# Attention in a decoder trunk: one chain for both key heads of a tile pair, with their 64-row score products issued in turn into two banks

## The chip, the cores and the metric

The kernel runs on one core of a Trainium2 chip. The metric is the device time of one execution in microseconds, as the median of several runs. The profile is of one such execution.

## What is computed

The reference is a trunk of two decoder layers over 256 tokens of width 1024. Each layer has a feed-forward block, a token mixer (a matrix-memory branch beside sliding-window attention), a second feed-forward block and a gated input embedding. The part that matters here is the attention of 16 query heads over 4 key heads, each of 64 features, with a window of 128 tokens and a sink logit per head:

```python
scores = jnp.einsum("bnqhgd,bnkhd->bnhgqk", qb, kw) * (A_HEAD_DIM ** -0.5)
scores = jnp.where(valid[None, :, None, None], scores, -jnp.inf)
mx = jnp.maximum(jnp.max(scores, axis=-1, keepdims=True), sink)
pr = jnp.exp(scores - mx)
den = jnp.sum(pr, axis=-1, keepdims=True) + jnp.exp(sink - mx)
attn = (pr / den).astype(v.dtype)
out = jnp.einsum("bnhgqk,bnkhd->bnqhgd", attn, vw)
```

Its output `ha` goes through the product with `w_branch_a` (called ya below), is gated, and is added to the other branch.

## The kernel before

Tokens stand in two tiles of 128 (t = 0, 1). Every float32 product is carried as three products of the high and low parts of its factors, in a form that TensorE takes at full pace: high x high, high x low, low x high. Weights come from memory in 1 MB loads, ScalarE casts a part of one to its high half (`wh<-raw`), VectorE subtracts that from the whole (`wl<-raw,wh`), and eight split parts make a ring. A ninth is split only when one is dropped.

TensorE, ScalarE, VectorE and the load queue issue in the order in which the program was written out. That order comes from `Trunk` and its estimate of time, `Clock`. The big products are cut into short steps, and ahead of each `tick` (line 195) moves on those background chains whose next stage is ready by the estimate, then splits another weight part. A chain is a generator that yields wherever what follows has to wait for what it issued. `XT.wait` (line 157), called ahead of a step that reads a transposed activation, finishes the chains that still have to write it: `finish` (line 220) then issues what is left of them one stage after the other, with nothing of the waiting product in between.

In the token mixer (`mix`, line 710) the order of the big products is: kvq (keys, values and queries), v, gt (a gate), `if` (16 products for the memory's gates), ya, and then z. Of the memory branch, the chains `scans` (line 913) and `decays` (line 1000) follow `if` and run beside ya: VectorE's gate instructions, five small transposes, and four sets `wt` of products, each with three exponentials `w` behind it. The product ya is issued in two halves by its k-tiles: the first half (96 products) reads the attention output of the pair p = 0, both token tiles, and the second half (96 products) that of the pair p = 1.

The attention itself is `Swa` (line 1080). The transposed queries and keys hold a pair p of key heads in one tile of 128 partitions: head g = 0 in rows 0 to 63, g = 1 in rows 64 to 127. `groups` (line 1154) starts one chain `group` per p, t and g, eight in a layer, in the order p, t, g, as soon as its inputs are there and fewer than ACTIVE + 1 of its list are alive. The list also holds the chain `groups` itself, so ACTIVE = 5 means that up to five groups are at work.

A group does this, each step on one engine:

1. TensorE, `scores`: a mask product of 128 rows and 512 columns opens a bank `sc`, then products of 64 rows follow, three per query head. For t = 0 a bank takes four query heads of 128 keys (12 products of 128 columns), for t = 1 two of 256 keys (6 products of 256 columns), twice.
2. VectorE takes the maximum `mx`, ScalarE the exponentials `pr` with their sums `dn`, VectorE and ScalarE the sink's part `es`, and ScalarE scales `pr` by the reciprocal.
3. For each key tile s: TensorE transposes four blocks of `pr` into a bank `tp`, ScalarE casts them to `ptd` (high), VectorE subtracts (low), TensorE multiplies with the values into the bank `ha` (three products of 512 columns).
4. Behind the last `ha` set of both g, ScalarE and VectorE split the result into the place of the queries, `qT`, from where ya reads it.

In the profile all these have the line of the issuing helper, L129, so that they are told apart by the names of their tiles.

Of the kernel before, what the change touches and what calls it, by code (L numbers as in the profile page):

```python
# [12 lines left out]
F32R = mybir.dt.float32r  # L13
BF16 = mybir.dt.bfloat16
AF = mybir.ActivationFunctionType
ALU = mybir.AluOpType
# [3 lines left out]
P = 128  # L20
# [29 lines left out]
class Part:  # L50
    """k k-tiles of n weight columns, from column c0 of the raw tile: split into high and low when fed."""
# [111 lines left out]
class Trunk:  # L163
    """Every float32 product x @ w is carried as xh @ wh + xh @ wl + xl @ wh, where
    xh is x rounded to float32r and xl = x - xh, which float32r holds exactly.

    TensorE, ScalarE and VectorE issue in the order written here. The products with the weights are cut into steps
    of about 1.3 us; before each, tick() splits weights that come later and moves the chains in the background
    (norms, transposes, attention) on, so that what TensorE meets next has been ready for a while."""
# [57 lines left out]
    def defer(self, fn, *args):  # L227
        """fn(*args), once what it reads is ready; what it yields, if anything, are stages of a chain."""
# [19 lines left out]
    def consts(self):  # L248
# [11 lines left out]
        def mask(out, base, step, channel):  # L260
            """0 where base + step * column + channel * row >= 0, else NEG."""
# [23 lines left out]
    def unit(self, w, c0, n=NB):  # L285
        """Registers columns c0..c0+n of w [1024, .]."""
# [7 lines left out]
    def halves(self, src):  # L294
        """Registers two units by halves of their k-tiles; src(u, h) is a list of (raw -> view, DRAM source)."""
# [11 lines left out]
    def prefetch(self, n=RAW, cut=False):  # L307
        """Issues loads until n raw tiles are under way (cut: each in two transfers)."""
# [12 lines left out]
    def feed(self, must=False):  # L321
        """Starts to split the next weight part if it is there and the queues are short enough, or if it must."""
# [34 lines left out]
    def need(self, part):  # L357
        """Has part split before a product with it is issued."""
# [52 lines left out]
    def project_T(self, unit, xT, base):  # L411
        """(x @ unit)^T -> PSUM banks [features, 2 * T], two feature tiles in each."""
# [43 lines left out]
    def transposes(self, src, n):  # L456
        """src [P, n*128] -> PSUM [P, n, 128]."""
# [28 lines left out]
    def first_gain(self, vec):  # L486
        """The same in PSUM: products with ones, which also have TensorE's clock up when the first rows arrive."""
# [33 lines left out]
    def first_norm(self, t, g, xT):  # L521
        """The norm of the input; the first weight part's split (entry) goes between its products and its copies."""
# [36 lines left out]
    def ffn(self, xT, wg, wu, wd, sink, first=6):  # L559
# [48 lines left out]
        def last_features(c0):  # L608
            """The last features' gate and up columns side by side in one stationary tile."""
# [100 lines left out]
    def mix(self, l, xT, sink):  # L710
        """ga, gm and the merged branches carry twice their values, which the sink's scale takes back."""
# [37 lines left out]
        def job_T(units, xT, base, use, before=None):  # L749
            """use(k, ps) takes the k-tiles k, k + 1 of the transposed product [features, 2 * T]."""  # L750
# [6 lines left out]
        def gate(c0):  # L757
            """tanh(gate / 2) by k-tiles, transposed."""
# [47 lines left out]
    def per_feature(self, l):  # L806
        """Per-partition columns: conv taps (k, tile), conv bias (tile), q and k gains (both halves)."""
# [60 lines left out]
class Mlstm:  # L868
    """Matrix memory in parallel form over two blocks of 128 tokens."""
# [7 lines left out]
    def prepare(self, w_in):  # L877
        """The loads for the gates."""
# [382 lines left out]
```

## Time and profile before

| | us |
|---|---|
| median of 3 runs | 1411.66 |
| lowest and highest run | 1410.39, 1412.22 |
| span of the profiled execution | 1409.6 |
| TensorE busy | 1394.8 |
| VectorE busy | 862.7 |
| ScalarE busy | 728.0 |
| TensorE in attention's score products, 192 of 64 rows (15.6 + 12.4) | 28.0 |
| TensorE in the 24 mask products | 9.4 |

The span runs from the first to the last instruction of the execution that the profiler took; the median is of other runs, timed as a whole. Busy times of matmuls overlap, since one starts while the one before it drains. What a matmul costs is therefore read from one start to the next, or from the chain of work that ended last, which counts each stretch of time once. A timeline row gives the start, the length, the engine, the instruction with its tiles and shapes, and the count, with the idle time ahead of it and who ended that in brackets.

### The profile page before, as it was taken

The page shows a single profiled execution, that of the slowest core. Times are in us where ns is not written, and L with a number is a line of the kernel's source. Part 1 is how long each engine was busy: PE and PEld are TensorE (multiplying, and loading weights), DVE is VectorE, ACT ScalarE, POOL GpSimd, SP SyncE. Part 2 cuts the span into 40 slices and gives each one's busy share as a digit, 9 for nine tenths or more (in the row PEclk, how much of TensorE's full clock was granted, in tenths as well). Part 3 has the DMA queues.
Part 4 walks back from the last instruction along what each step waited for, and adds up shares of the span by engine and source line. Part 5 has one row for each costly group of instructions (what it writes and reads, how often), then busy time and mean ns, then how long its engine had stood idle before and what let it go on. Part 6 is the DMA issues. An engine that isn't in the chain of part 4 may idle for free.

```text
span 1409.6 us, 21951 instructions
## 1 busy us (share of the span) xinstructions
PE 1394.8 (99%) x9064; PEld 1247.4 (88%) x9064; DVE 862.7 (61%) x1209; ACT 728.0 (52%) x1136; POOL 50.1 (4%) x78
## 2 busy tenths in 40 slices
PE   8999999999999999999999999999999999999998
PEld 6999877899999889988779998778998998999876
DVE  5656457655887665454575554675658876555544
ACT  5544346765655454443554444467646654544433
POOL 0000012000000000000000000120000000000000
PEclk9999999999999999999999999999999999999999
DMA  6665645354545565565456566443545544765651
GB/s 214 220 205 174 216 138 180 109 132 151 193 151 179 165 193 196 165 232 179 164 174 206 168 209 203 147 143 104 145 150 195 172 158 162 221 193 172 204 177 60
DMA packets 125830, 243.81 MB, mean 173 GB/s; under 512 B 14977, under 2 KB 23841, under 8 KB 125730
## 3 DMA queue, kind: packets, MB, share of 16 engines
q1 hardware_dynamic: 125730, 242.41, 53.6%
q8 instruction: 71, 1.16, 0.3%
q14 instruction: 29, 0.24, 0.1%
HBM read 241.34 MB, written 1.05 MB: 172 GB/s over the span
## 4 chain that ended last, share of the span: by engine, by line
PE 95%; DMA 2%; DVE 2%; ACT 1%; issue 0%; POOL 0%; SPq 0%; ACTq 0%
PE dn L129 17%; PE pg L129 15%; PE pu L129 14%; PE gt L129 7%; PE z L129 6%; PE gu L129 6%; PE kvq L129 5%; PE ya L129 3%; PE v L129 3%; PE ym L129 3%; PE og L129 3%; PE yo L129 3%; PE tp L129 3%; PE sc L129 2%; PE ha L129 1%; DVE wl L129 1%
## 5 line engine op out<-in xcount | busy, mean ns | idle before, releaser
L129 DVE TENSOR_TENSOR wl<-raw,wh 128x1024 fp32r<-128x1024 f32 x448 | 541.4, 1222 | 371.0 <-ACT wh L129 367.8
L129 ACT CAST wh<-raw 128x1024 fp32r<-128x1024 f32 x448 | 461.9, 1049 | 422.9 <-PE dn L129 92.4
L129 PE MATMUL dn<-wh,hid 128*128 128x512 f32 x688 | 219.2, 397 | 0.0
L129 PE MATMUL pg<-uT,wh 128*128 128x256 f32 x1088 | 194.7, 281 | 0.0
L129 PE MATMUL pu<-uT,wh 128*128 128x256 f32 x1088 | 193.8, 280 | 0.0
L129 PEld LDWEIGHTS pg<-uT,wh 128*128 128x128 f32 x1088 | 167.2, 189 | 0.2
L129 PEld LDWEIGHTS pu<-uT,wh 128*128 128x128 f32 x1088 | 167.2, 189 | 0.0
L129 PEld LDWEIGHTS dn<-wh,hid 128*128 128x128 f32 x688 | 129.2, 188 | 32.4 <-issue 2.9
L129 PE MATMUL pu<-uT,wl 128*128 128x256 f32 x544 | 153.3, 282 | 0.0
L129 PE MATMUL pg<-uT,wl 128*128 128x256 f32 x544 | 153.3, 282 | 0.0
L129 PE MATMUL dn<-wl,hid 128*128 128x512 f32 x352 | 140.6, 399 | 0.0
L129 PEld LDWEIGHTS pg<-uT,wl 128*128 128x128 f32 x544 | 102.3, 188 | 0.0
L129 PEld LDWEIGHTS pu<-uT,wl 128*128 128x128 f32 x544 | 102.3, 188 | 0.0
L129 PE MATMUL gt<-uT,wh 128*128 128x256 f32 x512 | 93.7, 284 | 0.0
L129 PE MATMUL z<-uT,wh 128*128 128x256 f32 x512 | 92.3, 282 | 0.0
L129 PE MATMUL gu<-wh,uT 128*128 128x512 f32 x256 | 83.9, 404 | 1.7 <-ACT uT L129 1.7
L129 PEld LDWEIGHTS dn<-wl,hid 128*128 128x128 f32 x352 | 66.1, 188 | 19.5 <-issue 5.3
L129 PEld LDWEIGHTS gt<-uT,wh 128*128 128x128 f32 x512 | 78.9, 189 | 1.3
L129 PEld LDWEIGHTS z<-uT,wh 128*128 128x128 f32 x512 | 78.6, 188 | 0.2
L129 PE MATMUL z<-uT,wl 128*128 128x256 f32 x256 | 72.0, 281 | 0.0
L129 PE MATMUL gt<-uT,wl 128*128 128x256 f32 x256 | 71.9, 281 | 0.0
L129 PE MATMUL kvq<-wh,uT 128*128 128x512 f32 x192 | 63.4, 400 | 0.0
(188 smaller groups left out, 2057.4 us busy)
## 6 DMA issues: line engine op xcount, KB each, us to landing
raw<-in_w_in_dram SPq DMA_DIRECT2D x60, 1024.0 KB, 4.9
raw<-in_ffn_w_up_dram SPq DMA_DIRECT2D x40, 1024.0 KB, 5.0
raw<-in_ffn_w_down_dram SPq DMA_DIRECT2D x40, 1024.0 KB, 5.1
raw<-in_ffn_w_gate_dram SPq DMA_DIRECT2D x39, 1024.0 KB, 5.1
raw<-in_w_branch_a_dram SPq DMA_DIRECT2D x16, 512.0 KB, 5.8
raw<-in_w_branch_m_dram SPq DMA_DIRECT2D x8, 1024.0 KB, 4.9
raw<-in_w_out_dram SPq DMA_DIRECT2D x8, 1024.0 KB, 4.9
raw<-in_ple_gate_w_dram SPq DMA_DIRECT2D x8, 1024.0 KB, 5.9
```

The lines of the kernel that those rows point to most:

```text
L129: return issue(*args, **kw)
```

## The change

The two chains of a tile pair, one per key head, become one chain `pair` per p and t, four in a layer. Its score products for the two heads are issued in turn: first the two mask products, then for each query head and each of the three products the one of g = 0 (rows 0 to 63) into the first bank, the one of g = 1 (rows 64 to 127) into the second. The maxima, exponentials, sums and scalings of the two heads follow in one chain, the heads one after the other, and the transposes and `ha` sets go g by g and s by s. ACTIVE goes from 5 to 2. As the chain `groups` is in the list still, up to two pairs are at work. The number of instructions stays. Comments are dropped throughout.

```diff
-ACTIVE = 5              # attention groups at work at a time
+ACTIVE = 2
...
-                for g in range(2):
-                    while sum(c in tr.bg for c in chains) > ACTIVE:
-                        yield
-                    chains.append(tr.start(self.group(t, p, g, acc)))
-                    self.haT.written(chains[-1], 4 * p, 4, t)
+                while sum(c in tr.bg for c in chains) > ACTIVE:
+                    yield
+                chains.append(tr.start(self.pair(t, p)))
+                self.haT.written(chains[-1], 4 * p, 4, t)
...
         def scores(j0):
-            ps = tr.bank("sc").rearrange("p (j s) -> p j s", j=per)
-            mask = tr.band[:, 2 * P - S :]
-            nc.tensor.matmul(ps, tr.identb, mask[:, None, :].to_broadcast([P, per, S]), start=True, stop=False,
-                             skip_group_check=True)
+            ps = [tr.bank("sc").rearrange("p (j s) -> p j s", j=per) for _ in range(2)]
+            for g in range(2):
+                nc.tensor.matmul(ps[g], tr.identb, mask, start=True, stop=False, skip_group_check=True)
             for j in range(per):
                 for x, y in ((0, 0), (0, 1), (1, 0)):
-                    nc.tensor.matmul(ps[:, j, :], self.qT[x](4 * p + j0 + j, tok, p=rows), self.kT[rows, y, p, :S],
-                                     start=False, stop=x == 1, skip_group_check=True)
+                    for g in range(2):
+                        nc.tensor.matmul(ps[g][:, j, :], self.qT[x](4 * p + j0 + j, tok, p=rows[g]),
+                                         self.kT[rows[g], y, p, :S], start=False, stop=x == 1, skip_group_check=True)
             return ps
...
         for j0 in range(0, 4, per):
             ps = scores(j0)
+            js = slice(j0, j0 + per)
             yield
-            yield from weights(j0, ps)
...
+            for g in range(2):
+                nc.vector.tensor_reduce(mx[g][:, js], ps[g], axis=AX.X, op=ALU.max)
+                nc.vector.scalar_tensor_tensor(mx[g][:, js], mx[g][:, js], -0.125, self.nsink[:, hd[g]][:, js],
+                                               op0=ALU.mult, op1=ALU.min)
+                yield
+                for j in range(per):
+                    i = j0 + j
+                    nc.scalar.activation(pr[g][:, i, :], ps[g][:, j, :], AF.Exp, scale=0.125, bias=mx[g][:, i : i + 1],
+                                         accum_out=den[g][:, i : i + 1])
...
+        out, n, total = None, 0, 2 * (t + 1)
+        for g in range(2):
             for j in range(4):
-                nc.tensor.transpose(ps[:, j * P : (j + 1) * P], pr[:, j, s * P : (s + 1) * P], tr.ident)
+                nc.scalar.mul(pr[g][:, j, :], pr[g][:, j, :], den[g][:, j : j + 1])
             yield
-            ptd = tr.slot("ptd", F32R)[:, : 2 * NB].rearrange("p (x n) -> p x n", x=2)
-            yield from tr.splitting(ptd[:, 0], ptd[:, 1], ps)
-            yield
...
+            for s in range(t + 1):
+                ps = tr.bank("tp")
+                for j in range(4):
+                    nc.tensor.transpose(ps[:, j * P : (j + 1) * P], pr[g][:, j, s * P : (s + 1) * P], tr.ident)
+                yield
+                ptd = tr.slot("ptd", F32R)[:, : 2 * NB].rearrange("p (x n) -> p x n", x=2)
+                yield from tr.splitting(ptd[:, 0], ptd[:, 1], ps)
+                yield
+                out = out or tr.bank("ha")
+                tr.mm3(out, self.vpad[s, 0][:, 2 * p + g, :], self.vpad[s, 1][:, 2 * p + g, :], ptd[:, 0], ptd[:, 1],
+                       n == 0, n == total - 1)
+                n += 1
```

The first place is TensorE's order at the first scores of the first layer (p = 0, t = 0). Before, one head's bank `sc` is opened by its mask and filled:

```order
L129 MATMUL kvq_2218<-wh_2137,uT_113 128x512
L129 LDWEIGHTS identb
L129 MATMUL sc_2308<-band,identb 128x512
L129 MATMUL sc_2308<-kT_1989,qT_130 128x128 x2
L129 MATMUL sc_2308<-kT_1989,qT_132 128x128
```

Now two banks are opened, and the products alternate between them:

```order
L129 MATMUL kvq_2218<-wh_2137,uT_113 128x512
L129 LDWEIGHTS identb
L129 MATMUL sc_2312<-band,identb 128x512
L129 LDWEIGHTS identb
L129 MATMUL sc_2313<-band,identb 128x512
L129 MATMUL sc_2312<-kT_1989,qT_130 128x128
L129 MATMUL sc_2313<-kT_1989,qT_130 128x128
```

The second bank's mask product has moved ahead of the first bank's score products, and each of these has one of the other rows behind it.

The second place is TensorE's order around the last `ha` set of the first layer, which ends the chain p = 1, t = 1. The tiles `qT_130` and `qT_132` hold the output of p = 0 (high and low), `qT_131` and `qT_133` that of p = 1. Before, the set stands within the first half of ya, 42 of whose products are ahead of it and 54 behind:

```order
L129 MATMUL ya_3178<-qT_132,wh_2946 128x256
L129 MATMUL ya_3178<-qT_130,wl_2947 128x256
L129 MATMUL ha_3075<-ptd_3201,vpad_1987 128x512 x3
L129 MATMUL ya_3179<-qT_130,wh_2946 128x256
L129 MATMUL ya_3179<-qT_132,wh_2946 128x256
```

Now four sets of transposes and four `ha` sets stand between the last `wt` set and the second half of ya:

```order
L129 MATMUL wt_3309<-mask_st,identb 128x128
L129 MATMUL tp_3324<-ident,pr_3079 128x128 x4
L129 MATMUL ha_3332<-ptd_3329,vpad_1985 128x512 x3
L129 MATMUL tp_3336<-ident,pr_3079 128x128 x4
L129 MATMUL ha_3332<-ptd_3341,vpad_1987 128x512 x3
L129 MATMUL tp_3351<-ident,pr_3080 128x128 x4
L129 MATMUL ha_3332<-ptd_3356,vpad_1985 128x512 x3
L129 MATMUL tp_3362<-ident,pr_3080 128x128 x4
L129 MATMUL ha_3332<-ptd_3367,vpad_1987 128x512 x3
L129 MATMUL ya_3115<-qT_131,wh_2896 128x256
L129 MATMUL ya_3115<-qT_133,wh_2896 128x256
```

The whole end of that chain has moved behind the first half of ya. Its first scores have moved too: before, the last two score banks of the layer were issued among the products of gt; now one pair of banks stands right behind `if` and the other among the first half of ya.

The third place is ScalarE's order for the same chain end. Before, the last cast of `ptd` and the cast of the result stand between the memory's gates and weight parts:

```order
L129 CAST ptd_3201<-tp_3185 128x512
L129 ACTIVATE gates_3175<-gates_3175 4x256
L129 ACT_TABLE_LOAD
L129 ACTIVATE gates_3175<-gates_3175 4x256
L129 CAST wh_3233<-raw_3097 128x1024
L129 CAST qT_131<-ha_3075 128x4x128
```

Now the chain's scaling, four casts and the cast of the result follow the last `w` exponentials:

```order
L129 ACTIVATE w_3300<-wt_3309,gcols_3178 128x128 x3
L129 ACTIVATE pr_3079<-pr_3079,dn_3083 128x256 x4
L129 CAST ptd_3329<-tp_3324 128x512
L129 CAST ptd_3341<-tp_3336 128x512
L129 ACTIVATE pr_3080<-pr_3080,dn_3084 128x256 x4
L129 CAST ptd_3356<-tp_3351 128x512
L129 CAST ptd_3367<-tp_3362 128x512
L129 CAST qT_131<-ha_3332 128x4x128
```

They have moved behind the `w` exponentials of all four `wt` sets, and the scaling of the second head stands between the casts. The second layer's order is like the first's in all three places.

More of the change, by code (lines that the diff above doesn't have):

```diff
@@ L1154, in groups @@
     def groups(self, chains):
-        tr, acc = self.tr, {}
+        tr = self.tr
         for p in range(2):
@@ L1160, in groups, with pair @@
                     yield
[L1161 to L1167 removed]
+                while sum(c in tr.bg for c in chains) > ACTIVE:
+                    yield
+                chains.append(tr.start(self.pair(t, p)))
+                self.haT.written(chains[-1], 4 * p, 4, t)
+    def pair(self, t, p):
         tr, nc = self.tr, self.nc
@@ L1171, in group @@
         per = NB // S
-        rows = slice(g * AD, (g + 1) * AD)
         tok = slice(t * P, (t + 1) * P)
-        hd = slice(4 * (2 * p + g), 4 * (2 * p + g) + 4)
-        pr = tr.slot("pr")[:, : 4 * S].rearrange("p (j s) -> p j s", j=4)
-        mx, den, es = tr.col("mx", 4), tr.col("dn", 4), tr.col("es", 4)
+        rows = [slice(g * AD, (g + 1) * AD) for g in range(2)]
+        hd = [slice(4 * (2 * p + g), 4 * (2 * p + g) + 4) for g in range(2)]
+        pr = [tr.slot("pr")[:, : 4 * S].rearrange("p (j s) -> p j s", j=4) for _ in range(2)]
@@ L1178, in scores @@
+        mx, den, es = ([tr.col(n, 4) for _ in range(2)] for n in ("mx", "dn", "es"))
+        mask = tr.band[:, 2 * P - S :][:, None, :].to_broadcast([P, per, S])
         def scores(j0):
-            ps = tr.bank("sc").rearrange("p (j s) -> p j s", j=per)
-            mask = tr.band[:, 2 * P - S :]
-            nc.tensor.matmul(ps, tr.identb, mask[:, None, :].to_broadcast([P, per, S]), start=True, stop=False,
-                             skip_group_check=True)
+            ps = [tr.bank("sc").rearrange("p (j s) -> p j s", j=per) for _ in range(2)]
+            for g in range(2):
+                nc.tensor.matmul(ps[g], tr.identb, mask, start=True, stop=False, skip_group_check=True)
@@ L1205, in group @@
+        for g in range(2):
+            nc.vector.tensor_tensor(es[g], mx[g], self.sink[:, hd[g]], op=ALU.add)
         yield
-        nc.scalar.activation(es, es, AF.Exp)
+        for g in range(2):
+            nc.scalar.activation(es[g], es[g], AF.Exp)
         yield
-        nc.vector.tensor_tensor(den, den, es, op=ALU.add)
-        nc.vector.reciprocal(den, den)
+        for g in range(2):
+            nc.vector.tensor_tensor(den[g], den[g], es[g], op=ALU.add)
+            nc.vector.reciprocal(den[g], den[g])
@@ L1210, in group @@
         yield
-        for j in range(4):
-            nc.scalar.mul(pr[:, j, :], pr[:, j, :], den[:, j : j + 1])
-        yield
-        total = 2 * (t + 1)
-        for s in range(t + 1):
-            ps = tr.bank("tp")
-            for j in range(4):
-                nc.tensor.transpose(ps[:, j * P : (j + 1) * P], pr[:, j, s * P : (s + 1) * P], tr.ident)
-            yield
-            ptd = tr.slot("ptd", F32R)[:, : 2 * NB].rearrange("p (x n) -> p x n", x=2)
-            yield from tr.splitting(ptd[:, 0], ptd[:, 1], ps)
-            yield
-            if (t, p) not in acc:
-                acc[t, p] = [tr.bank("ha"), 0]
-            out, n = acc[t, p]
-            acc[t, p][1] += 1
-            tr.mm3(out, self.vpad[s, 0][:, 2 * p + g, :], self.vpad[s, 1][:, 2 * p + g, :], ptd[:, 0], ptd[:, 1],
-                   n == 0, n == total - 1)
@@ L1235, in tile_trunk @@
+        yield
+        yield from tr.splitting(self.haT[0](4 * p, tok, 4), self.haT[1](4 * p, tok, 4),
+                                out.rearrange("p (j t) -> p j t", j=4))
 @with_exitstack
```

18 lines of the change are left out of this document (3 added, 15 removed).

## The prediction, made before the changed kernel ran

> **What bounds the kernel now.** I read the page first: the busy times and the chain of work that ended last.
>
> ```profile
> PE 1394.8 (99%) x9064; PEld 1247.4 (88%) x9064; DVE 862.7 (61%) x1209; ACT 728.0 (52%) x1136; POOL 50.1 (4%) x78
> PE 95%; DMA 2%; DVE 2%; ACT 1%; issue 0%; POOL 0%; SPq 0%; ACTq 0%
> ```
>
> TensorE sets the end. A busy share over the whole span says nothing of one stage, so the second view was the busy time by stretches of the attention part of the first layer (columns: stretch, its length, busy time of PE, PEld, DVE, ACT, POOL, then the granted clock, DMA share and GB/s).
>
> ```profile
> 230.00:260.00 30.00, 30.00 (x165) 23.44 (x164) 21.36 (x47) 21.24 (x61) 3.54 (x10) 1.00 0.42 139
> 260.00:290.00 30.00, 30.00 (x175) 24.77 (x173) 17.81 (x32) 23.65 (x64) 0.00 (x0) 1.00 0.28 76
> 290.00:320.00 30.00, 30.00 (x239) 29.14 (x239) 18.82 (x34) 19.75 (x37) 0.95 (x1) 1.00 0.61 150
> 320.00:345.00 25.00, 25.00 (x190) 22.07 (x189) 14.45 (x21) 12.84 (x22) 0.00 (x0) 1.00 0.46 152
> ```
>
> TensorE has no gap here at all. So two things count and nothing else does: TensorE time that the change saves in this part, and TensorE idle time that it makes there. Both go into the end one for one. By the order of instructions the streams of TensorE are alike ahead of the first scores of a layer and again from the first z product on, so everything happens between these two places, once per layer.
>
> **Part 1, the score products in turn.** The timeline of TensorE, around the first four score banks (start, length, instruction, count), its weight loads in the same place, and the chain of work that ended last:
>
> ```profile
> 235.17 0.39 PE L129 MATMUL sc<-band,identb 128*128 128x512 bf16 x1
> 235.49 1.55 PE L129 MATMUL sc<-kT,qT 64*128 64x128 f32 x12
> 236.97 0.39 PE L129 MATMUL sc<-band,identb 128*128 128x512 bf16 x1
> ...
> 239.58 0.39 PE L129 MATMUL sc<-band,identb 128*128 128x512 bf16 x1
> 239.90 0.97 PE L129 MATMUL sc<-kT,qT 64*128 64x256 f32 x6
> 240.81 0.39 PE L129 MATMUL sc<-band,identb 128*128 128x512 bf16 x1
> ```
>
> ```profile
> 235.49 1.41 PEld L129 LDWEIGHTS sc<-kT,qT 64*128 64x128 f32 x12 [0.23 <-ACT sq L129]
> ```
>
> ```profile
> 235.33 3.52 PE sc L129 x26
> 239.74 2.37 PE sc L129 x14
> 467.77 21.54 PE yo L129 x93
> ```
>
> A 128-column product costs (236.97 - 235.49) / 12 = 0.123 us, a 256-column one (240.81 - 239.90) / 6 = 0.152. The mask product ahead of them takes 0.32 to the next start (235.17 to 235.49); a full-array product of 512 columns in a row of its like takes 21.54 / 93 = 0.232, so 0.09 is the price of going from 128 rows to 64. Two groups of token tile 0 take 3.52 us on the chain, two half-groups of token tile 1 take 2.37.
>
> The trace of before has no two neighbouring products on different rows of the array, so what turn by turn brings is bounded. If two neighbours run at once, a pair costs what one costs: 0.23 + 0.32 + 12 x 0.123 = 2.03 for token tile 0, which saves 1.49; 0.23 + 0.32 + 6 x 0.152 = 1.46 for token tile 1, which saves 0.91. Ahead of the ya products there are per layer two of each: 4.8 us, 9.6 for both layers. If the weight loads still go one behind the other, at the pace of the row of loads (twelve in 1.41 us with the last one's 0.19 in it, 0.11 to 0.12 each), the pair for token tile 0 stays at 0.55 + 24 x 0.123 = 3.50 and the other becomes 0.55 + 12 x 0.118 = 1.97: per layer 2 x 0.02 + 2 x 0.40, 1.7 for both. Below zero: if each change of rows cost the 0.09 of the change from 128 rows, 2 x 24 x 0.09 + 2 x 12 x 0.09 = 6.5 per layer would be added. Nothing excludes that, but both kinds are already 64-row products, so I keep it as a rival only. No row lies nearer to one of the gaining ends, so I take their middle, 5.7 us. The Trainium skill, "TensorEngine Tiling (Array Packing)", Key Properties, says that tiles work independently and can load weights and multiply in parallel, while changing the tiling mode drains TensorE. By this rule the gain would be the upper end and the sum 3.9 us lower; the 0.09 us at the mask agrees with its drain, and no run here shows the parallel part yet.
>
> The two pairs of the last chain stand between the ya products, where TensorE waits for others in any case (part 2), so I count nothing for them (at most 4 x 0.91 = 3.6 for both layers).
>
> **Part 2, the order that follows.** With two chains at a time, the last one (p = 1, token tile 1) starts its scores only after the `if` products, and the second half of ya needs its result. Before, the last ha set stood among the first half of ya, with 54 ya products behind it. In the changed order four steps stand with nothing between them: 4 transposes, ha, 4 transposes, ha, and so on, then ya. Each step is a chain through three engines. Its prices, from the timelines of PE, ACT and DVE (in brackets the idle time before and who ended it), and what TensorE itself needs, from the chain:
>
> ```profile
> 314.17 0.60 PE L129 MATMUL tp<-ident,pr 128*128 128x128 f32 x4
> ...
> 319.55 0.86 PE L129 MATMUL ha<-ptd,vpad 128*128 128x512 f32 x3
> ```
>
> ```profile
> 296.26 0.59 ACT L129 CAST qT<-ha 128x512 fp32r<-128x512 f32 x1 [2.33 <-PE ha L129]
> ...
> 306.84 0.56 ACT L129 CAST ptd<-tp 128x512 fp32r<-128x512 f32 x1
> ...
> 314.86 0.59 ACT L129 CAST ptd<-tp 128x512 fp32r<-128x512 f32 x1 [1.57 <-PE tp L129]
> ...
> 320.45 0.59 ACT L129 CAST qT<-ha 128x512 fp32r<-128x512 f32 x1 [1.33 <-PE ha L129]
> ```
>
> ```profile
> 296.87 0.69 DVE L129 TENSOR_TENSOR qT<-ha,qT 128x512 fp32r<-128x512 f32 x1 [2.77 <-ACT qT L129]
> ...
> 307.44 0.69 DVE L129 TENSOR_TENSOR ptd<-tp,ptd 128x512 fp32r<-128x512 f32 x1 [0.85 <-ACT ptd L129]
> ```
>
> ```profile
> 313.64 0.69 PE ha L129 x3
> 314.33 0.44 PE tp L129 x4
> ```
>
> From the first transpose to the cast 0.69 (314.17 to 314.86), cast to subtraction 0.60 (306.84 to 307.44), subtraction 0.69: at 1.98 the second of the three ha products can go, and with two at 0.23 the next transposes start at 2.44. TensorE's own work in that is 0.69 + 0.44 = 1.13, so a step idles 1.31, four of them 5.2 us. Behind the last one comes the cast of the output, 0.90 after the first of three unbroken products (319.55 to 320.45), so 0.44 after the third, then 0.61 to the subtraction (296.26 to 296.87) and 0.69 of it: 1.98 + 0.23 + 0.44 + 0.61 + 0.69 = 3.95 from the step's start, of which 2.44 is in the step: 1.5 more. Between the second and the third step ScalarE also scales the second head's four weights; its 1.71 (below) fits beside the subtraction and ha but for about 0.2.
>
> What stands ahead of the first step:
>
> ```profile
> 330.62 1.05 PE wt L129 x4
> ```
>
> ```profile
> 292.22 1.71 ACT L129 ACTIVATE pr<-pr,dn 128x256 f32<-128x256 f32 x4 [0.97 <-DVE dn L129]
> ...
> 331.71 0.88 ACT L129 ACTIVATE w<-wt,gcols 128x128 f32<-128x128 f32 x3 [2.36 <-PE wt L129]
> ```
>
> In the changed order TensorE issues the last wt set and then the transposes; ScalarE stands at three w exponentials of that wt, which start as the set ends (331.67, 331.71) and take 0.88, and behind them four scalings, 1.71. The last transpose waits for the last scaling, so TensorE idles at least 0.04 + 0.88 + 1.71 less three transposes at 0.11, 2.3. ScalarE comes there with much else behind it (eight exponentials of scores, nine of w, four weight casts within the 96 ya products), so it may be later still; I take 2.7 and up to 5.
>
> At the start of ya the first product needs the subtraction of the ha set that stands right behind `if`. VectorE has gate work and a weight subtraction in front of it, and ScalarE a table load in front of the next cast:
>
> ```profile
> 313.68 0.47 DVE L129 TENSOR_SCALAR gates<-if,m_igate_b 4x256 f32<-4x256 f32 x1 [2.12 <-PE if L129]
> ...
> 315.92 1.21 DVE L129 TENSOR_TENSOR wl<-raw,wh 128x1024 fp32r<-128x1024 f32 x1
> ```
>
> ```profile
> 316.46 1.28 ACT L129 ACT_TABLE_LOAD   x1
> ```
>
> From the end of `if`: 0.2, 2.24 for the gates, 1.21 and 0.69 make 4.3, against TensorE's own two ha sets, four transposes and a score pair, 2 x 0.69 + 0.44 + 2.37 = 4.2 (3.3 if the pair overlaps). With the next ha set behind the table load this is between 0 and 2 us; I take 1.
>
> So a layer idles 1 + 2.7 + 5.2 + 0.2 + 1.5 = 10.6 us, both 21.2. It isn't given back: in before no stretch of this part has a wait that an earlier TensorE stall could fill, and the ring of eight weight parts only stands full when ya goes on. The count of all instructions stays, the weight transfers (SP's queue) only stand a little earlier against them, and VectorE and ScalarE have room (61% and 52%), so the moved max, exponential and scaling work costs nothing outside the waits above.
>
> **The sum.** The profiled execution has a span of 1409.6; the runs' median of 1411.66 is 2.1 more. Span: 1409.6 + 21.2 - 5.7 = 1425.1; time: 1427.2.
>
> **The rivals.** *The products don't overlap, chance 0.20.* For it: the pace of 0.123 at 128 columns looks like the loads' pace, not the columns'. Gain 1.7 instead of 5.7: 1431.2.
>
> *The clock falls in the wait, 0.14.* The last TensorE product of before starts at 1404.15; the granted clock is still full in the next stretch and half in the one after:
>
> ```profile
> 1404.15 0.39 PE L129 MATMUL pg<-wh,uT 128*128 128x512 f32 x1
> ```
>
> ```profile
> 1406.00:1408.00 2.00, 0.00 (x0) 0.00 (x0) 0.62 (x1) 0.00 (x0) 0.00 (x0) 1.00 0.26 103
> 1408.00:1409.60 1.60, 0.00 (x0) 0.00 (x0) 0.00 (x0) 0.00 (x0) 0.00 (x0) 0.52 0.09 35
> ```
>
> So about 3.5 us idle halve it. The wait ahead of the first step is 2.3 to 5. Price: the parts of four steps on the chain doubled, 4 x (0.44 + 0.46) = 3.6, and some 3.5 us of ya at half speed, 1.8: 5.4 per layer, 10.8 for both: 1438.0. Against it: 2.7 is under 3.5, and each step has products. The Trainium skill, "TensorE: Matmul & The Clock Gate", Part 1, gives an idle window of about 3.4 us for the fall and as long a busy one for the rise; the end of the trace agrees with the first.
>
> *Changing rows drains the array, 0.06.* 13 us are added, none gained: 1411.66 + 21.2 + 13 = 1445.9.
>
> *Faster, 0.06.* The pairs overlap everywhere, also between the ya products: 9.6 + 3.6 = 13.2. That decides once a layer idles less than 6.6, so with ScalarE ahead of TensorE at the first step (no 2.7, no 1) and steps shorter by a third, as would be if the 0.69 to the cast were mostly ScalarE's own lateness there: 2 x 4.7 - 13.2 = -3.8, 1407.9. Against it: ScalarE's 1.57 of idle time ended by just those transposes. In between, no change has 0.04.
>
> **How the numbers follow.** The forecast (waits of 10 us a layer, part of the overlap) has 0.50 and gives 1427.2. Low end: no extra lateness, 2 x (2.3 + 5.2 + 1.5) = 18.0 less 9.6 gives 1420; with steps a third shorter and all overlap counted it goes to about 1415, which I take. High end: 2 x (5 + 6.9 + 2) = 27.8 without gain, 1439.5; the clock's 1438.0 lies in it; I take 1441. Within 0.2% (2.8 us, about what measurements of this kernel can tell) lies only the in-between case: same 0.04, faster 0.06, slower 0.90.
>
> **What would show it.** Right: TensorE's waits list shows tp for ACT, ha for DVE and ya for DVE, some 10 us a layer between `if` and z, where before lists none; a pair for token tile 0 takes 2.0 (overlap) or 3.5 us (none). Wrong: those waits sum to under 4 us a layer, or the pair takes over 3.6, or the granted clock leaves 1.00 there.

## The result, and the profile after

| | before | after |
|---|---|---|
| median (lowest to highest), us | 1411.66 (1410.39 to 1412.22) | 1429.59 (1428.48 to 1430.36) |
| span of the profiled execution, us | 1409.6 | 1426.7 |
| mean granted clock there | 0.999 | 0.985 |

The changed kernel is slower: the medians differ by 17.9 us, or 1.3%, where 15.5 us had been forecast. The ratio on record is 1.0116, with a 95% interval of 1.0095 to 1.0137, which holds the medians' 1.0127. The forecast of 1427.2 was close, but two of its parts were wrong by some 8 and 10 us, in opposite directions. The mean clock already points to one of them.

The page of the changed kernel (busy times, then the granted clock in 40 slices):

```profile
PE 1400.3 (98%) x9064; PEld 1245.5 (87%) x9064; DVE 862.1 (60%) x1209; ACT 727.5 (51%) x1136; POOL 51.8 (4%) x78
PEclk9999999997999999999999999999889999999999
```

TensorE is busy 5.5 us longer with the same instructions, and the clock falls in slice 10 (321 to 357 us) and in slices 29 and 30: the ends of the two layers' attention. These are its waits (waiting engine and tile, engine and tile waited for, sum, count, longest; two at the start of the kernel are left out):

```profile
PE ha L129 <- ACT ptd L129: 5.4, 8, 0.7
PE tp L129 <- DVE xn L129: 3.8, 2, 2.4
PE tp L129 <- ACT pr L129: 2.7, 2, 1.4
PE tp L129 <- DMA p<-in_p_dram: 2.5, 2, 2.2
...
PE ya L129 <- DVE qT L129: 1.6, 2, 0.8
PE ya L129 <- ACT qT L129: 1.4, 2, 0.7
```

The tiles are those of the prediction: `tp` waits for the scaling, `ha` for the casts, `ya` for the output. But they sum to 5.4 + 2.7 + 1.6 + 1.4 = 11.1 us, 5.5 a layer where 10 had been expected. The rest hides in busy time, as the timeline of TensorE at the end of the chain shows:

```profile
321.49 1.52 PE L129 MATMUL tp<-ident,pr 128*128 128x128 f32 x4 [1.37 <-ACT pr L129]
323.68 1.95 PE L129 MATMUL ha<-ptd,vpad 128*128 128x512 f32 x3 [0.68 <-ACT ptd L129]
325.43 1.05 PE L129 MATMUL tp<-ident,pr 128*128 128x128 f32 x4
327.16 1.95 PE L129 MATMUL ha<-ptd,vpad 128*128 128x512 f32 x3 [0.68 <-ACT ptd L129]
...
336.73 1.30 PE L129 MATMUL ya<-qT,wh 128*128 128x256 f32 x2 [0.68 <-ACT qT L129]
```

A step takes 327.16 - 323.68 = 3.48 us, not 2.44. Three unbroken `ha` products had taken 0.86; these take 1.95. The busy times by stretches say why (the granted clock is the third number from the end):

```profile
315.00:320.00 5.00, 5.00 (x30) 3.07 (x29) 2.36 (x4) 4.61 (x18) 0.00 (x0) 1.00 0.13 49
320.00:325.00 5.00, 2.75 (x9) 1.34 (x7) 1.40 (x6) 3.21 (x10) 0.00 (x0) 0.81 0.67 210
325.00:330.00 5.00, 4.28 (x13) 2.54 (x11) 0.69 (x1) 2.20 (x6) 0.00 (x0) 0.50 0.01 3
330.00:335.00 5.00, 3.70 (x9) 2.13 (x10) 1.38 (x2) 1.16 (x2) 0.00 (x0) 0.50 0.00 0
335.00:340.00 5.00, 4.18 (x15) 3.17 (x16) 0.69 (x1) 0.59 (x1) 0.00 (x0) 0.50 0.00 0
340.00:345.00 5.00, 5.00 (x43) 5.00 (x43) 2.33 (x3) 1.64 (x2) 0.00 (x0) 0.98 0.00 0
```

The clock is half from 323.1 to 340.2 us, through all four steps and the first ya products, and again for 20.5 us in the second layer. Products at half clock look like work in a list of waits, so that list understates the loss.

The score products went the other way. The timeline at the first pair, and the pairs on the chain of work that ended last:

```profile
234.83 0.61 PE L129 MATMUL sc<-band,identb 128*128 128x512 bf16 x2
235.37 1.55 PE L129 MATMUL sc<-kT,qT 64*128 64x128 f32 x24
236.85 0.50 PE L129 MATMUL kvq<-wh,uT 128*128 128x512 f32 x1
```

```profile
234.99 1.93 PE sc L129 x26
...
237.82 1.35 PE sc L129 x14
...
275.21 1.93 PE sc L129 x25
...
311.13 1.33 PE sc L129 x14
```

24 products now take 236.85 - 235.37 = 1.48 us, what 12 took before: the overlap is full. On the chain a pair for token tile 0 costs 1.93 us and one for token tile 1 1.35. The forecast's bounds (2.03 and 3.50, 1.46 and 1.97) were added up from one start to the next; read in that way the first two pairs take 236.85 - 234.83 = 2.02 and 239.10 - 237.66 = 1.44. In the profile of before the layer's eight groups take 16.2 us on the chain, now 2 x 1.93 + 4 x 1.34 = 9.2. That is 7.0 a layer, 14 for both, of which 3.7 lie in the last chain, for which nothing had been counted. (One of its pairs stands behind `if`, off the chain; it is taken to be as long as the other.) The Trainium skill, "TensorEngine Tiling (Array Packing)", Key Properties, says that tiles work independently and can load weights and multiply in parallel; the trace agrees, with 24 products in 1.48 us.

So there are three things to settle by experiment. Is the loss all in the order that ACTIVE = 2 makes? Is the gain due to the other rows, to the other bank, or to both? And how much is the clock, and what makes it fall, since TensorE stood idle nowhere in this part for 3.5 us?

One thing is needed to read the times below: on the chips of the experiments the clock also fell in some executions of the kernel before, which took 1410.2 to 1419.9 us at mean clocks of 1.000 to 0.992. Each ratio is against its runs on the same chip; the arithmetic between kernels uses executions at a clock of 1.00 where it says so.

### The profile page after: what moved, and what is told of

The parts are those of the page before. It is cut to its first block, busy times and chain, and to the rows that moved or that the text cites. A ratio compares the mean times of both kernels' runs of the same rounds, so it can differ in the third digit from the quotient of the medians.

```text
span 1426.7 us, 21932 instructions
## 1 busy us (share of the span) xinstructions
PE 1400.3 (98%) x9064; PEld 1245.5 (87%) x9064; DVE 862.1 (60%) x1209; ACT 727.5 (51%) x1136; POOL 51.8 (4%) x78
## 3 DMA queue, kind: packets, MB, share of 16 engines
q8 instruction: 71, 1.16, 0.3%
## 4 chain that ended last, share of the span: by engine, by line
PE 95%; DMA 2%; DVE 1%; ACT 1%; issue 0%; SPq 0%; ACTq 0%
PE dn L129 17%; PE pg L129 15%; PE pu L129 14%; PE gu L129 7%; PE z L129 6%; PE gt L129 6%; PE kvq L129 5%; PE ya L129 4%; PE ym L129 3%; PE v L129 3%; PE yo L129 3%; PE og L129 3%; PE tp L129 3%; PE ha L129 2%; PE sc L129 1%; DMA raw<-in_ffn_w_gate_dram 1%
```

## Experiments: the order

**Four chains at a time.** The changed kernel with one number changed:

```diff
-ACTIVE = 2
+ACTIVE = 4
```

> The changed kernel with ACTIVE = 4, so that all four pairs of a layer may be at work and the last one's scores are issued among the gt products again. Theory A (the loss is the order: the last chain stands alone ahead of the second half of ya, and the half clock follows from that idle time; the overlap itself saves 16.2 - 9.3 = 6.9 us a layer): no waits of TensorE between the first scores and z, clock 1.00 there, 1411.7 - 13.9 = 1397 to 1400 us. Rival B (the pair chain itself makes the wait, since its two heads go one after the other): 1420 us or more, with the same waits ahead of ya. Rival C (the overlap is given back elsewhere, in ScalarE or in PSUM banks): 1408 to 1412 us.

Measured: 1401.23 us (1399.57 to 1403.66), ratio 0.9894 (0.9879 to 0.9910). The slowdown is gone, and the kernel is faster than before. An execution at a clock of 1.00 took 1399.57. All of the last chain but its last `ha` set is done while ya's first half runs. That set stands behind the half, and the waits of TensorE between 300 and 340 us are down to these:

```profile
PE ya L129 <- ACT qT L129: 0.7, 1, 0.7
PE ya L129 <- DVE qT L129: 0.3, 1, 0.3
```

This is the whole sum without the chain's end: 1411.66 less 14 of overlap, plus twice 1.0, gives 1399.7. The loss of the change lay in ACTIVE = 2, not in the pairing. The profile, which is of the slowest of the four executions (1403.66 us), still has half clock behind these waits, for 3.4 us in the first layer and 6.8 in the second.

**A quarter of z ahead of ya.** 96 of a layer's 384 z products, which need nothing from the attention, are put ahead of ya, so that the chain's end stands among them and the first ya products (both layers, with ACTIVE = 4):

```diff
+        rec.qk_job(w_in, 0, 0)
...
-        for part in range(2):
-            rec.qk_job(w_in, part, 0)
+        rec.qk_job(w_in, 1, 0)
```

> ACTIVE = 4, in turn, and the first z product (96 products with uT, which waits for no attention) is issued ahead of ya instead of behind it, so that the last ha set stands 100 products ahead of the second half of ya. Theory A: the 1.0 us a layer that TensorE waited for ACT and DVE at ya is gone, and with it the windows of half clock there (1 in layer 1, 2 in layer 2): 1395 to 1398 us. Rival G (the half clock comes from the wt products beside, not from the wait): half clock still, 1399 to 1402 us. Rival H (the memory branch loses its cover when z moves): over 1402 us.

Measured: 1396.75 us (1395.66 to 1397.82), ratio 0.9862 (0.9840 to 0.9884). No wait of ya is left in the list, and the clock is half for only one stretch of 3.4 us, at 700.6, in the input embedding. This is the best version, and it beats both kernels.

## Experiments: what overlaps

**The banks one after the other.** The changed kernel, but each bank filled on its own behind the two masks:

```diff
-            for j in range(per):
-                for x, y in ((0, 0), (0, 1), (1, 0)):
-                    for g in range(2):
+            for g in range(2):
+                for j in range(per):
+                    for x, y in ((0, 0), (0, 1), (1, 0)):
```

> The changed kernel, but each bank's products issued in one go, first those of head g = 0, then those of g = 1; the rest of the order as in the changed kernel. Theory A (neighbours on different rows run at once): the pairs go back to 3.4 and 2.3 us; those ahead of ya count in full, 2 x (2 x 1.5 + 2 x 0.95) = 9.8 us, the others by up to 3.8: 1439 to 1443 us. Rival (the saving came from two mask products in a row and fewer changes between 128 and 64 rows, 0.09 us each): at most 1432 us.

Measured: 1434.89 us (1432.51 to 1435.64), ratio 1.0132 (1.0115 to 1.0149), 5.3 above the changed kernel. Neither expectation held, and the chain shows the reason:

```profile
234.23 2.88 PE sc L129 x26
...
238.01 1.70 PE sc L129 x14
```

Without turns a pair should have taken 3.5; it takes 2.88. The recorded starts are 0.11 us apart, except at the seam, where seven follow each other after 0.05 to 0.06 us in the mean: the last four or so products of the first head and the first four of the second lie in one another. The records don't name the head, but products of this width on the same rows start 0.11 us apart everywhere else, so the close starts must alternate between the rows. By this reading TensorE starts products on the other rows ahead of products on its present rows that are written before them, about four places ahead. A third of a bank's twelve overlaps without turns, if nothing with 128 rows stands at the seam. With the four pairs a layer that stand well ahead of ya, 2 x (2 x 0.95 + 2 x 0.35) = 5.2, near the 5.3 measured. That it is so near is in part luck: in the profiles the two stretches from the first scores to z are 7.2 us longer, with half clock for 3.4 us more in the first layer, and the rest of the program is 3.2 us shorter.

The same with ACTIVE = 4, where the order costs nothing:

> ACTIVE = 4 and each bank's products in one go: the pair chain with neither the turn by turn nor the late last chain. Theory A: within 3 us of the kernel before, 1409 to 1414 us, no waits ahead of ya. Rival B (the pair chain costs by itself): 1416 us or more.

Measured: 1408.88 us (1406.87 to 1417.82), ratio 0.9962 (0.9942 to 0.9983). At a clock of 1.00 it took 1407.0, 7.4 above the 1399.57 of ACTIVE = 4; all pairs by the chain give 2 x (2 x 0.95 + 4 x 0.35) = 6.6.

**A mask between the heads.** With ACTIVE = 4, the second mask product moved behind the first head's products, so that a product of 128 rows stands at the seam, as before the change:

```diff
-            for g in range(2):
-                nc.tensor.matmul(ps[g], tr.identb, mask, start=True, stop=False, skip_group_check=True)
             for g in range(2):
+                nc.tensor.matmul(ps[g], tr.identb, mask, start=True, stop=False, skip_group_check=True)
                 for j in range(per):
```

> ACTIVE = 4, and the two heads' scores apart as in the kernel before: mask and products of g = 0, then mask and products of g = 1, so that a 128-row product stands between the two row halves. Theory A' (products of the two row halves run at once, in turn for the whole pair, and at the seam for about four products ahead where no 128-row product stands between): no two starts closer than 0.1 us, a pair at 3.5 and 2.3 us again, and over the run with ACTIVE = 4 in turn all of 2 x (2 x 1.59 + 4 x 1.0) = 14 us, 1412 to 1416 us. Rival (the early starts in the run with whole banks came from something else, as the order of loads): a pair under 3.0 us here too, at most 1410 us.

Measured: 1425.52 us (1423.19 to 1431.80), ratio 1.0073 (1.0047 to 1.0099). The pairs came out as expected, at the price of before; the time did not:

```profile
235.64 3.52 PE sc L129 x26
...
240.05 2.37 PE sc L129 x14
...
249.98 7.46 PE sc L129 x40
```

A mask at the seam is enough to undo all of the overlap. By the chain, the pairs are 0.64 and 0.67 longer than in the run before this one: 1407.0 + 2 x (2 x 0.64 + 4 x 0.67) = 1415, so some 10 us are unexplained by the products. The clock was half for 30.7 us, which can cost up to half of that, 15.4 us, if TensorE has no wait to fill there. This is where it first fell:

```profile
250.45:253.86 3.41, 3.41 (x27) 2.81 (x26) 0.00 (x0) 2.08 (x5) 0.00 (x0) 1.00 0.03 5
253.86:257.27 3.41, 3.41 (x13) 2.63 (x13) 1.84 (x5) 0.00 (x0) 0.00 (x0) 0.50 0.00 0
```

TensorE had been busy for every one of the 3.41 us ahead of the fall, with nothing but masks and 64-row products. No idle time is needed; this is taken up below.

**The other bank or the other rows.** With ACTIVE = 4, in each layer's first pair the products of one head alternate between two banks, on the same rows, and then those of the other head; the four masks are half as wide:

```diff
...
+            for g in range(2):
+                for h in range(2):
+                    nc.tensor.matmul(banks[g][h], tr.identb, mask[:, :2], start=True, stop=False,
+                                     skip_group_check=True)
+                for j in range(2):
+                    for x, y in ((0, 0), (0, 1), (1, 0)):
+                        for h in range(2):
+                            nc.tensor.matmul(banks[g][h][:, j, :], self.qT[x](4 * p + 2 * h + j, tok, p=rows[g]),
...
```

> ACTIVE = 4, products in turn, but the first pair of each layer (p = 0, token tile 0) has its heads one after the other and each head's products alternate between two banks with the same rows. Theory A' (it is the other rows, not the other bank): starts 0.11 us apart within a head, so the two heads' 24 products take 2.6 to 3.0 us, against 1.48 in turn by rows. Rival F (another bank is enough): starts in pairs and 1.5 us. Elsewhere as with ACTIVE = 4.

One execution: 1406.76 us. The first pair of each layer, on the chain:

```profile
235.69 3.68 PE sc L129 x28
```

```profile
930.39 3.52 PE sc L129 x28
```

In the first layer the clock falls to half at 238.90, within the pair. At full clock, in the second layer, the pair takes the 3.52 us of before, and within a head no two starts are closer than 0.108 us. The bank brings nothing; the rows do.

## Experiments: the clock

**Unread products against the fall.** The changed kernel with 25 mask products a layer whose results nobody reads: 8 ahead of the first transposes, 3 behind each set, 5 ahead of ya:

```diff
+        last = p == 1 and t == 1
+        full = tr.band[:, None, :].to_broadcast([P, 2, 2 * P])
+
+        def warm(bank, times):
+            for _ in range(times if last else 0):
+                tr.tc.nc.tensor.matmul(bank.rearrange("p (j s) -> p j s", j=2), tr.identb, full, start=True, stop=True,
+                                       skip_group_check=True)
...
+                if n == 0:
+                    warm(ps, 8)
...
+                if last:
+                    spare = tr.bank("warm")
+                    warm(spare, 3)
...
+        if last:
+            warm(spare, 5)
```

> The changed kernel with extra mask products that nothing reads, in TensorE's idle time of the last chain of each layer: eight ahead of its first transposes, three behind each set of transposes, five ahead of the second half of ya (25 a layer, 0.23 us each). The order of all else is the same. Theory A (the half clock costs 5 to 6 us a layer on top of the waits): the clock stays at 1.00, a step takes 2.4 to 2.5 us instead of 3.47, 1417 to 1421 us. Rival D (the steps are bound by ScalarE and VectorE, the half clock costs nothing): 1428 to 1432 us, whatever the clock shows. Rival E (the products come too late or are too thin to hold the clock): clock 0.50 still, 1429 us or more.

Measured: 1418.29 us (1417.27 to 1420.63), ratio 1.0030 (1.0015 to 1.0046), with the clock at 1.00 throughout in the profile. With more work the kernel is 11.3 us faster than the changed one (9.9 between the two profiled executions). It also shows the waits at full clock. One step on the chain:

```profile
324.91 0.45 PE tp L129 x4
325.38 0.59 ACT ptd L129
326.00 0.70 DVE ptd L129
326.75 0.73 PE ha L129 x2
327.48 0.49 PE tp L129 x4
```

2.57 us from one set of transposes to the next, for a forecast of 2.44. Transposes, cast, subtraction and two `ha` products, each waiting for the one before: the step was read rightly.

**Only the eight ahead of the first step:**

> The changed kernel with only the eight unread mask products ahead of the last chain's first transposes (8 of the 25 of the run with all of them). It tells where the clock falls. Theory J (the wait ahead of the first step lets it fall, the steps themselves keep what they find): clock 1.00, 1418 to 1421 us. Rival K (the steps, with 1.3 us idle in each 2.4, let it fall by themselves): clock 0.50 from the second or third step on, 1425 to 1430 us.

Measured: 1424.04 us (1421.10 to 1424.87), ratio 1.0055 (1.0037 to 1.0073). The first fall is put off from 323.1 to 326.3 us in the first layer, but the steps by themselves then let the clock fall, for 13.7 and 17.1 us. Neither expectation was met fully: the long wait is not the only cause, and where it is filled the loss is smaller.

**A count of the use.** With ten profiles at hand I took the moments at which the granted clock changes. In each profile they lie on a grid of 3.413 us (323.09, 715.62 and 1026.24 in the changed kernel are 115 and 91 such stretches apart), so every stretch of the grid can be looked at. For each I summed the products' columns, at the 0.232 us per 512 columns of the chain, each product weighed by its rows over 128, so that one of 64 rows counts half. With the two runs below there are twelve profiles. They give, for stretches at full clock from the first clock record (13 to 17 us) to the last product:

| use of a stretch, columns x rows | stretches | followed by half clock |
|---|---|---|
| under 0.35 | 17 | 17 |
| 0.35 to 0.45 | 21 | 6 |
| over 0.45 | 4794 | 0 |

Counted by columns alone, without the rows, nothing separates them: 12 of the 82 stretches between 0.35 and 0.70 were followed by a fall. The stretch ahead of the fall in the changed kernel (319.68 to 323.09) has a use of 0.10. A step at full clock has 0.93 us of products in 2.44 to 2.57, 0.36 to 0.38: on the edge. At half clock it has 0.93 in 3.48, 0.27, and stays there until ya runs. And a score pair as before the change, 12 + 12 products of 64 rows and two masks, has 1.16 us of full use in 3.52, 0.33: when a stretch of the grid falls on it whole, as at 235.49 in the profile with the same rows and at 250.45 with the mask between, the clock falls. That would also explain why the kernel before varies from 1410 to 1420, but this is not shown, since no profile of one of its slower executions was taken. Two runs test the count.

**One unread product per step instead of three** (17 a layer):

> The changed kernel with unread mask products as in the run warm, but one behind each set of transposes instead of three (8 ahead of the first set and 5 ahead of ya as there, about 17 a layer). Theory U (use): the clock is set anew every 3.41 us by how much TensorE worked in the 3.41 us before, a product counting its columns times its rows over 128. In the profiles so far every such stretch with under a third of the full pace (512 columns in 0.232 us) was followed by half clock, none with over 0.44. A step of 4 transposes and 3 ha products is 0.93 us of products; with one of 0.23 more, in a step of about 2.5 us, the use is 0.46: the clock stays at 1.00 and the time is that of warm or a little below, 1417 to 1420. Rival V (gaps): the clock falls because TensorE stands still about 1 us in each step; one product more leaves a gap of that size: half clock in both layers, 1423 to 1430.

Measured: 1420.07 us (1417.77 to 1421.50), ratio 1.0043 (1.0027 to 1.0058). The time is that of the upper end expected for the use, 1420. TensorE now waits in each step, and the clock holds. These are two stretches of this profile's grid, with a use of 0.37 and 0.46; the first lies where both outcomes occur, so the run speaks against the gaps rather than for an exact bound:

```profile
321.22:324.63 3.41, 2.59 (x10) 1.15 (x9) 0.69 (x1) 1.56 (x4) 0.00 (x0) 1.00 0.82 289
324.63:328.04 3.41, 2.64 (x14) 1.37 (x12) 0.69 (x1) 2.44 (x6) 0.00 (x0) 1.00 0.00 0
```

**All 25, but on 32 rows instead of 128**, so that they take as long and count a quarter (against the run with 25):

```diff
-                tr.tc.nc.tensor.matmul(bank.rearrange("p (j s) -> p j s", j=2), tr.identb, full, start=True, stop=True,
+                tr.tc.nc.tensor.matmul(bank.rearrange("p (j s) -> p j s", j=2), tr.identb[:32], full[:32], start=True, stop=True,
...
```

> The run warm (25 unread mask products a layer in the same places), but each of them on 32 rows instead of 128, with the same 512 columns, so that TensorE is busy as long but works on a quarter of the rows. Theory U (use, a product counting columns times rows): the first 3.41 us hold 8 products of 0.23 at a quarter and four transposes, 0.46 + 0.23 = 0.7 us or a use of 0.2, so the clock falls ahead of the steps; a step then has 0.93 + 0.17 in about 3.6 us, 0.31, and it stays at half: 1427 to 1433. Rival B (busy time): what counts is whether TensorE runs anything: the clock stays at 1.00 as in warm, 1417 to 1421.

Measured: 1435.46 us (1434.29 to 1435.76), ratio 1.0147 (1.0119 to 1.0175). The stretch ahead of the fall, with a use of 0.24, and the two behind it:

```profile
319.40:322.81 3.41, 3.34 (x16) 1.25 (x14) 1.25 (x5) 3.16 (x12) 0.00 (x0) 1.00 0.45 106
322.81:326.22 3.41, 3.41 (x10) 1.84 (x10) 0.69 (x1) 0.58 (x1) 0.00 (x0) 0.50 0.53 202
326.22:329.64 3.42, 3.42 (x10) 1.57 (x9) 0.69 (x1) 2.19 (x5) 0.00 (x0) 0.50 0.00 0
```

TensorE is busy 3.34 of 3.41 us, and the clock falls; with one product of 128 rows per step it is busy 2.59 and 2.64 of 3.41, and the clock stays. It is not the idle time that counts but columns times rows. The time is above the expected 1427 to 1433, since the clock was half for 20.5 and 23.9 us, longer than in the changed kernel, and the unread products too take twice as long there.

## Why the prediction was right in its number and wrong in two parts

In the terms of its own sum, with the same 1411.66 as start:

| term, both layers | forecast | measured | from |
|---|---|---|---|
| score products | -5.7 | -14 | chain, 16.2 to 9.2 a layer |
| waits at full clock | +21.2 | +20.6 | warm: 1418.29 + 14 - 1411.66 |
| half clock | 0 | +11.3 | changed kernel less warm |
| sum | 1427.2 | 1429.6 | |

Two of the measured terms are differences of medians from different chips, and the sum comes out by construction. The profiles check them. From the first score bank of a layer to its first z product the two layers take 107.8 and 107.8 us before, 110.8 and 110.9 with the unread products, and 115.2 and 116.2 in the changed kernel. So the half clock costs 4.4 + 5.3 = 9.7 us there, and the waits 6.1 + 14 = 20.1. The remaining 1.3 us of the difference of the spans lie outside these stretches.

- **The waits: right.** With the clock kept up, the two layers lose 20.6 us by the medians and 20.1 by the profiles, if the unread products cost nothing there. In the first layer of that run it can be read directly: from 319.72, the start of the unread products behind the last `wt` set, to the second ya product at 334.05 are 14.3 us, of which four steps' own work is 4 x 1.13 and one ya product 0.12. That leaves 9.7; the forecast for the same part was 2.7 + 5.2 + 0.2 + 1.5 = 9.6. Ahead of the first ya half TensorE waited 0.8 a layer, forecast 1. That the list shows only 5.5 a layer comes from the half clock, in which the products fill part of their own wait.
- **The overlap: right in its mechanism, mis-sized.** "No row lies nearer to one of the gaining ends, so I take their middle, 5.7 us" failed: the upper end was the true one, with 10.3 us instead of 9.6 for the pairs ahead of ya. Nearly all of the 0.7 between them is a slip in the working and no further overlap: it subtracted a length from start to start (2.03, measured 2.02) from one on the chain (3.52), where the same two groups count 0.09 less than from start to start (235.17 to 238.78, 3.61). And "I count nothing for them", of the last chain's two pairs, failed as well: 3.7 us. One of the pairs stands among ya products and not in a wait; the other stands ahead of ya, whose wait the sum holds with the pair already overlapped. The argument for the lower end, that 0.123 us is the pace of the loads, was true of loads on the same rows only: in the changed kernel two loads start 3 ns apart. The rival "the products don't overlap" fell with it, and so did "changing rows drains the array": the 23 changes of rows among a pair's 24 products cost nothing that can be seen.
- **The clock: wrong.** It was kept as a rival at 0.14, and came true. The step that failed is "about 3.5 us idle halve it", with its conclusion "2.7 is under 3.5, and each step has products". TensorE's longest idle time here was 1.37 us. What the end of the trace showed was one case of low use, taken for a rule on idle time. The price was about right: 5.4 per layer, 10.8 for both, where the medians give 11.3 and the profiles 9.7. The Trainium skill, "TensorE: Matmul & The Clock Gate", Part 1, has a free-running window of 3413 ns, which the grid agrees with; it has the fall after an idle window, and there the measurement decides: windows with 100% of busy time were followed by half clock when their use was under 0.35.
- **The first step's wait: right in its cause, a little shorter.** From the end of the `wt` set at 320.1 to the last transpose at 322.68 are 2.6 us, less three transposes 2.2, at the low end of the forecast's 2.3 to 5, of which it took 2.7. ScalarE's rows show the queue that was named: the `w` exponentials, then the scalings.

```profile
319.10 0.88 ACT L129 ACTIVATE w<-wt,gcols 128x128 f32<-128x128 f32 x3
...
320.16 0.88 ACT L129 ACTIVATE w<-wt,gcols 128x128 f32<-128x128 f32 x3
320.92 1.70 ACT L129 ACTIVATE pr<-pr,dn 128x256 f32<-128x256 f32 x4
```

- **By its own test of being wrong**, "the granted clock leaves 1.00 there", the forecast's case did not happen. Full overlap, the forecast's waits and the rival's clock together would have given 1411.66 + 21.2 - 14 + 10.8 = 1429.7. That the number 1427.2 was close is luck: an under-counted gain and a left-out loss nearly cancelled.

## What to carry to other kernels

Two 64-row products on different halves of the rows run at once if they follow each other closely and no product on all rows stands between them; a chain that is made longer for this needs enough other chains at work, or its end stands bare. Before a dependent chain of small products is left alone on TensorE, sum its columns times rows per 3.4 us: under 0.35 of the pace, and in some cases up to 0.41, the price of the wait includes half clock for the chain itself, and it does not show in a list of waits. Give such a place a product that needs nothing from it, real work such as a quarter of z here.

## What the runs showed that was not expected

- The clock follows the use of the array, columns times rows, in free-running stretches of 3.41 us: all 17 stretches under 0.35 were followed by half clock, and none of 4794 over 0.45. A pair of score banks as before the change, 64-row products of 128 columns and their masks one behind the other, has 0.33.
- TensorE starts products on the other 64 rows some four places ahead of products written before them: 24 products in two blocks took 2.44 us, not 2.96.
- Two products in turn start 3 to 4 ns apart, their weight loads too, so the pair costs what one costs: 0.123 us at 128 columns.
- Unread products made the kernel faster: 25 a layer, some 10 us.
